# Value weights' high parts, and a third of the low parts, kept in the low 16 KB that a dead activation leaves

## The chip, the cores and the metric

The kernel runs on one core of a Trainium2 chip. The metric is the device time of one execution in microseconds (us). Three runs of the kernel before gave 1288.02, 1288.10 and 1289.45 us; their median is 1288.1 us.

## The reference

The reference is two transformer blocks over one sequence of 256 tokens, 1024 wide, in float32. The first block has sliding-window attention, a retention branch and a gated feed-forward. The second has a gated spatial unit, banded chunk attention and a PEER feed-forward: each token picks 16 of 16384 experts in each of 8 heads. Only that last part matters here. In the reference it is

```python
u = jnp.take(expert_u, eidx, axis=0)
h = jax.nn.gelu(jnp.einsum('thkd,td->thk', u, xb))
vv = jnp.take(expert_v, eidx, axis=0)
return jnp.einsum('thk,thkd->td', (g * h.astype(jnp.float32)).astype(xb.dtype), vv)
```

## The kernel before

The kernel doesn't gather experts. It computes the hidden value of every expert for every token, multiplies by a matrix that is zero where an expert was not picked, and multiplies with all of the value weights. So the PEER part is two dense layers of 128 blocks, each block with 128 experts and one 128x1024 weight tile (512 KB). The first layer (`first_layer`, L110 to L112) leaves its result in `S`, 128 blocks of 128 experts by 256 tokens. The second layer (`second_layer`, L1065) sums over the experts into four PSUM banks.

Every float32 matmul is made of three matmuls in `fp32r`. A weight is split in a high part (`whi`, made on ACT by a rounding copy, L95) and a low part (`wlo`, the rest, made on DVE, L96), an activation likewise. High by high, high by low and low by high are added up in PSUM.

In a matmul one operand is loaded into the array (the stationary one, `lhsT`, LDWEIGHTS, engine row PEld), and the other streams past it (the moving one, `rhs`). Which is which differs by stage:

- `gemm_t` (most of the program, the first PEER layer too): the weights are stationary, the activations move, 256 columns a matmul.
- `gemm_n` (some projections of both blocks): the activations are stationary, the weights move, 512 columns a matmul.
- `second_layer`: the split of `S` (tiles `keys` and `q`) is stationary, the value weights move, 512 columns a matmul. A block is 12 matmuls: for each of two token halves, `whi` by `keys`, `wlo` by `keys` and `whi` by `q`, each over two column halves. So the high part moves in 8 of them and the low part in 4.

The tiles lie along the partition, which holds 224 KB. Pools opened with the default side "right" lie at its top, the others at its bottom. As the program is built, the weights of this stage lie at the top: three buffers of `whi` from 184 KB, three of `wlo` from 196 KB, four of `raw` (the loaded weight) from 208 KB. The tiles `keys` (two) and `q` (three) lie from 178 KB. At the bottom, from 18.75 KB to 34.75 KB, lies the pool `xb`: the tiles `xbl` and `xbh`, the low and high part of the input of the first PEER layer. They are read for the last time by the last matmuls of that layer. The activations of the earlier stages (`acth`, `actl`) lie from 34.75 KB to 66.75 KB.

What sets the order: the Tile framework schedules each engine's instructions ahead of time and gives each engine a fixed list, which it works off in order. `unit` (L77) traces a weight's load, ACT copy and DVE subtraction with a raised priority, so that they are placed early, as far as a free buffer can be had for them at that place. A load is issued on SP's queue, and waits for the DVE subtraction that read the same `raw` buffer four weights before. At the seam between the layers ACT has four kinds of work in one list: weight splits (L95), the gelu of the last pair of first-layer blocks (L1003 and L1006), and the splits of `S` into `keys` (L154). PE's block j of the second layer needs `keys` and `q` of block j, and there are two `keys` buffers, so that the split of block j waits for block j-2 on PE.

Of the kernel before, what the change touches and what calls it, by code (L numbers as in the profile page):

```python
# [8 lines left out]
F32R = mybir.dt.float32r  # L9
# [34 lines left out]
class Net:  # L44
# [29 lines left out]
            self.wraw = self.pool(name + "r", raw, stack)  # L74
        self.wpools.append(self.pool(name + "p", parts, stack))

    def unit(self, src, n, pieces=1, engine=None, between=None):  # L77
        with self.tc.high_priority(offset=AHEAD):
            return self.unit_(src, n, pieces, engine, between)

    def unit_(self, src, n, pieces, engine, between):
        nc = self.nc
        self.turn += 1
        wpar = self.wpools[self.turn % len(self.wpools)]
        raw = self.wraw.tile([128, 1024], F32, name="raw")
        hi = wpar.tile([128, 1024], F32R, name="whi")
        lo = wpar.tile([128, 1024], F32R, name="wlo")
        for i in range(pieces):
            s = slice(i * n // pieces, (i + 1) * n // pieces)
            nc.sync.dma_start(out=raw[:, s], in_=src[:, s])  # L90
            if between and i:
                between(i)
        for i in range(pieces):
            s = slice(i * n // pieces, (i + 1) * n // pieces)
            self.last_copy = nc.scalar.activation(hi[:, s], raw[:, s], AF.Copy).ins  # L95
            low = (engine or nc.vector).tensor_tensor(out=lo[:, s], in0=raw[:, s], in1=hi[:, s].bitcast(F32),  # L96
                                                      op=OP.subtract)
            if engine is None:
                self.last_low = low.ins
        return hi, lo  # L100
# [616 lines left out]
    def peer(self, st, x3, h, acc):  # L717
        nc, a, tc = self.nc, self.a, self.tc
# [296 lines left out]
        def fetch(j):  # L1015

            C = gp.tile([128, 4, 128], F32, name="C", bufs=3)
            i = nc.gpsimd.dma_start(out=C, in_=cview[:, j:j + 4]).ins
            for o in put_by:
                tc.add_manual_dep(i, o.name, after, reason="all heads have been added")  # L1020
            return C

        def apply(j, C):
            with tc.issue_after(self.last_low):
                nc.vector.tensor_tensor(out=S[:, j:j + 4, TH:], in0=S[:, j:j + 4, TH:], in1=C, op=mult)
# [34 lines left out]
        def second_layer(j, tb, w, s, dhs):  # L1060
            ts = slice(tb * 128, tb * 128 + 128)
            for dh in dhs:
                for left, right, first, end in ((0, 0, j == 0, False), (0, 1, False, False), (1, 0, False, j == 127)):
                    for d in dh:
                        nc.tensor.matmul(banks[tb][d], lhsT=s[left][:, ts], rhs=w[right][:, d * 512:d * 512 + 512],  # L1065
                                         start=first, stop=end)

        held = []
        for j in range(128):
            w = self.unit(a["peer_v"][j], 1024)  # L1070
            s = [qp.tile([128, T], F32R, tag=t, name=t, bufs=n) for t, n in (("keys", 2), ("q", 3))]
            self.split(S[:, j], s[0], s[1])
            if j < 126:
                for tb in range(2):
                    second_layer(j, tb, w, s, ((0, 1),))
            else:
                held.append((j, w, s))
            if j % 4 == 0 and j < 124:
                apply(j + 4, fill.pop(0))
                if j < 116:  # L1080
                    fill.append(fetch(j + 12))
            if j == 120:
                groups.close()
                with tc.using_default_side("right"):
                    x3 = self.pool("x3", 1).tile([128, 2, D], F32, name="x3")
                nc.sync.dma_start(out=x3, in_=x3t.rearrange("b t d -> t b d"))
# [94 lines left out]
```

## Time and profile before

| | us |
|---|---|
| median of three runs | 1288.1 |
| the profiled execution | 1288.32 |
| its span | 1286.5 |
| PE busy | 1276.2 |
| DVE busy | 904.6 |
| ACT busy | 719.0 |
| the second PEER layer, first to last matmul start | 934.20 to 1282.15 |

The profile is one execution. The span is from the first to the last thing it shows; what lies outside of it is 1.8 us here. Engines are PE (matmul), PEld (loading the stationary operand), DVE, ACT, POOL and SP (which issues the loads). A timeline row has the start in us, the time it took in us, the engine, the line, the operation, and what is written and read. In brackets stands how long the engine was idle before it, and whom it waited for. PE's matmuls overlap in the rows, since each is shown until its last result is out. So the pace of PE is read from the distance of their starts, not from the time that one takes.

### The profile page before, as it was taken

Reading aid. Unit: us, or ns where it says so; the run is one execution under the profiler, and the core shown is the slowest. Engines: PE = TensorE matmul, PEld = TensorE weight load, DVE = VectorE, ACT = ScalarE, POOL = GpSimd, SP = SyncE. Lnnn points to the kernel's source line nnn. Section 1 sums busy time; section 2 is a strip of 40 time slices with the busy share of each in tenths; the row PEclk is TensorE's granted clock in tenths of the full one; section 3 lists DMA queues with packets and bytes.
Section 4 is the critical chain, followed back from the end, with each engine's and each line's share of the span. In section 5 each row is a group of like instructions: output and inputs, shape, how many; then the busy total and the mean of one; then the engine's idle time right before and its main releaser. Section 6 shows DMA issues by size and latency. Waiting matters only on the chain.

```text
span 1286.5 us, 23584 instructions
## 1 busy us (share of the span) xinstructions
PE 1276.2 (99%) x9125; PEld 1187.6 (92%) x9125; DVE 904.6 (70%) x1790; ACT 719.0 (56%) x1163; POOL 259.8 (20%) x173
## 2 busy tenths in 40 slices
PE   8999999999999999999999999999999999999998
PEld 8878999999999889999999999999988888888887
DVE  6767677766665887997995666666566666666665
ACT  5455545544454776645556666665555555555553
POOL 2000000000000000037787777770000000000000
PEclk8999999999999999999999999999999999999999
DMA  7745668966567444568777777775777777777764
GB/s 261 231 137 158 179 186 296 338 185 192 171 188 225 148 148 146 186 169 198 172 181 192 174 177 169 177 171 175 216 218 220 217 217 217 219 219 219 217 201 158
DMA packets 90928, 253.02 MB, mean 197 GB/s; under 512 B 26944, under 2 KB 28736, under 8 KB 90688
## 3 DMA queue, kind: packets, MB, share of 16 engines
q1 hardware_dynamic: 68816, 241.45, 61.0%
q0 software_dynamic: 20992, 8.46, 5.9%
q8 instruction: 71, 1.16, 0.4%
q10 hardware_dynamic: 1008, 1.61, 0.4%
q14 instruction: 41, 0.34, 0.1%
HBM read 240.93 MB, written 10.55 MB: 195 GB/s over the span
## 4 chain that ended last, share of the span: by engine, by line
PE 94%; DVE 3%; DMA 1%; issue 0%; POOL 0%; ACT 0%; SPq 0%; ACTq 0%; POOLq 0%; DVEq 0%
PE ax L1065 27%; PE mm L110 21%; PE mm L111 21%; PE mm L112 21%; DVE wlo L96 1%; PE ax L942 1%; DMA raw<-in_w_in_a_dram 1%; PE ax L888 0%; DMA xT<-in_xT_dram 0%; DVE itop L741 0%; PE ax L678 0%; PE ax L713 0%; PE ax L478 0%; PE ax L466 0%; PE ax L700 0%
## 5 line engine op out<-in xcount | busy, mean ns | idle before, releaser
L96 DVE TENSOR_TENSOR wlo<-raw,whi 128x1024 fp32r<-128x1024 f32 (+2 forms) x433 | 524.4, 1213 | 232.6 <-ACT whi L95 230.1
L95 ACT ACTIVATE whi<-raw 128x1024 fp32r<-128x1024 f32 (+3 forms) x439 | 457.6, 1045 | 306.2 <-PE mm L111 210.4
L110 PE MATMUL mm<-xbh,whi 128*128 128x256 f32 x1104 | 312.6, 283 | 0.0
L112 PE MATMUL mm<-xbh,wlo 128*128 128x256 f32 x1104 | 308.0, 279 | 1.7 <-DVE wlo L96 1.5
L111 PE MATMUL mm<-xbl,whi 128*128 128x256 f32 x1104 | 308.2, 279 | 0.0
L832 POOL DMA_INDIRECT cmat<-best,pos x128 | 232.1, 1813 | 219.1 <-DVE itop L741 155.4
L110 PE MATMUL mm<-acth,whi 128*128 128x256 f32 x848 | 240.2, 283 | 1.8 <-ACT acth L252 1.0
L111 PE MATMUL mm<-actl,whi 128*128 128x256 f32 x848 | 238.6, 281 | 0.7 <-DVE actl L253 0.6
L112 PE MATMUL mm<-acth,wlo 128*128 128x256 f32 x848 | 237.8, 280 | 0.0
L112 PEld LDWEIGHTS mm<-xbh,wlo 128*128 128x128 f32 x1104 | 207.4, 188 | 2.3 <-DVE wlo L96 2.3
L110 PEld LDWEIGHTS mm<-xbh,whi 128*128 128x128 f32 x1104 | 207.5, 188 | 0.2
L111 PEld LDWEIGHTS mm<-xbl,whi 128*128 128x128 f32 x1104 | 207.6, 188 | 0.0
L110 PEld LDWEIGHTS mm<-acth,whi 128*128 128x128 f32 x848 | 160.7, 190 | 2.9 <-ACT acth L252 1.2
L111 PEld LDWEIGHTS mm<-actl,whi 128*128 128x128 f32 x848 | 160.7, 189 | 1.6 <-DVE actl L253 1.5
L112 PEld LDWEIGHTS mm<-acth,wlo 128*128 128x128 f32 x848 | 160.8, 190 | 0.2 <-DVE wlo L96 0.2
L1065 PE MATMUL ax<-whi,keys 128*128 128x512 f32 x512 | 158.0, 389 | 0.0
L1065 PE MATMUL ax<-wlo,keys 128*128 128x512 f32 x512 | 157.9, 389 | 0.0
L1065 PE MATMUL ax<-whi,q 128*128 128x512 f32 x512 | 157.9, 389 | 0.0
L154 ACT ACTIVATE keys<-S 128x256 fp32r<-128x256 f32 x128 | 53.4, 418 | 151.4 <-PE ax L1065 151.4
L1065 PEld LDWEIGHTS ax<-wlo,keys 128*128 128x128 f32 x512 | 96.1, 188 | 20.0
L1065 PEld LDWEIGHTS ax<-whi,q 128*128 128x128 f32 x512 | 96.1, 188 | 19.9
L1065 PEld LDWEIGHTS ax<-whi,keys 128*128 128x128 f32 x512 | 96.0, 188 | 19.9
(282 smaller groups left out, 1409.1 us busy)
## 6 DMA issues: line engine op xcount, KB each, us to landing
raw<-in_peer_u_dram SPq DMA_DIRECT2D x128, 512.0 KB
raw<-in_peer_v_dram SPq DMA_DIRECT2D x128, 512.0 KB
raw<-in_w_in_b_dram SPq DMA_DIRECT2D x32, 512.0 KB
raw<-in_w_in_a_dram SPq DMA_DIRECT2D x31, 512.0 KB
raw<-in_w_gate_dram SPq DMA_DIRECT2D x22, 512.0 KB
raw<-in_w_up_dram SPq DMA_DIRECT2D x22, 512.0 KB
raw<-in_w_out_dram SPq DMA_DIRECT2D x16, 512.0 KB
cmat<-zero SPq DMA_DIRECT2D x16, 512.0 KB
```

The lines of the kernel that those rows point to most:

```text
L95: self.last_copy = nc.scalar.activation(hi[:, s], raw[:, s], AF.Copy).ins
L96: low = (engine or nc.vector).tensor_tensor(out=lo[:, s], in0=raw[:, s], in1=hi[:, s].bitcast(F32), op=OP.subtract)
L110: mm(ps, lhsT=left[0], rhs=right[0], start=first, stop=False)
L111: mm(ps, lhsT=left[0], rhs=right[1], start=False, stop=False)
L112: mm(ps, lhsT=left[1], rhs=right[0], start=False, stop=last)
L154: nc.scalar.activation(hi, src, AF.Copy)
L832: i = nc.gpsimd.indirect_dma_start(self.cmat, bass.IndirectOffsetOnAxis(ap=ps[:, hd, 1, k:k + 1], axis=0), bs[:, hd, 1, k:k + 1], None, co ...
L942: nc.tensor.matmul(C[:, t * 128:t * 128 + 128], lhsT=A[:, t], rhs=G[i][:, t], start=i == 0, stop=i == 1)
L1065: nc.tensor.matmul(banks[tb][d], lhsT=s[left][:, ts], rhs=w[right][:, d * 512:d * 512 + 512], start=first, stop=end)
```

## The change

From block 3 of the second layer on, the tiles for the weights' high part are no longer taken from the pool at the top. `xbl` and `xbh` are taken again under the name `under`, as two tiles of 2 x 1024 columns, which gives four places of 4 KB. The high part of block j goes to place j modulo 3. The low part goes to the fourth place when j is a multiple of 3, and to the three buffers of the pool otherwise.

```diff
-    def unit_(self, src, n, pieces, engine, between):
+    def unit_(self, src, n, pieces, engine, between, hi=None, lo=None):
...
-        hi = wpar.tile([128, 1024], F32R, name="whi")
-        lo = wpar.tile([128, 1024], F32R, name="wlo")
+        if hi is None:
+            hi = wpar.tile([128, 1024], F32R, name="whi")
+        if lo is None:
+            lo = wpar.tile([128, 1024], F32R, name="wlo")
...
         for j in range(128):
-            w = self.unit(a["peer_v"][j], 1024)
+            if j == 3:
+                under = [self.xbp.tile([128, 2, 1024], F32R, tag=t, name="under", bufs=1) for t in ("xbl", "xbh")]
+                under = [x[:, i] for x in under for i in range(2)]
+            place = {"hi": under[j % 3], "lo": None if j % 3 else under[3]} if j >= 3 else {}
+            w = self.unit(a["peer_v"][j], 1024, **place)
```

The order of ACT's list moves at the seam of the two layers. `whi_12041` is the high part of block 2, and `whi_12063` and `whi_12085` those of blocks 3 and 4; `gt_11985` and the row after it are the gelu of the last pair of the first layer; `keys_12046` is the split of `S` for block 2, `keys_12068` for block 3. Before:

```order
L95 ACTIVATE whi_12041<-raw_12040 128x1024
L1003 ACTIVATE gt_11985<-mm_11924 128x256
L1006 ACTIVATE S_6237<-mm_11924 128x2x128
L154 ACTIVATE keys_12046<-S_6237 128x256
L95 ACTIVATE whi_12063<-raw_12062 128x1024
L154 ACTIVATE keys_12068<-S_6237 128x256
L95 ACTIVATE whi_12085<-raw_12084 128x1024
```

With the change (its lines stand 2 lower in the file; `raw_12064`, `raw_12084` and `raw_12108` are the loaded weights of blocks 3, 4 and 5):

```order
L97 ACTIVATE whi_12041<-raw_12040 128x1024
L97 ACTIVATE under_12062<-raw_12064 128x1024
L97 ACTIVATE under_12062<-raw_12084 128x1024
L97 ACTIVATE under_12063<-raw_12108 128x1024
L1005 ACTIVATE gt_11985<-mm_11924 128x256
L1008 ACTIVATE S_6237<-mm_11924 128x2x128
L156 ACTIVATE keys_12046<-S_6237 128x256
L156 ACTIVATE keys_12068<-S_6237 128x256
```

The high parts of blocks 3, 4 and 5 have moved ahead of the gelu and of the split for block 2. Before, they stood behind it, one after each split.

On DVE, at the same seam, the rows behind the low part of block 2 (`wlo_12042`) were these before; `q_12047` is the low part of the split of `S` for block 2:

```order
L96 TENSOR_TENSOR wlo_12042<-raw_12040,whi_12041 128x1024
L1004 TENSOR_TENSOR S_6237<-S_6237,gt_11985 128x2x128
L155 TENSOR_TENSOR q_12047<-S_6237,keys_12046 128x256
L96 TENSOR_TENSOR wlo_12064<-raw_12062,whi_12063 128x1024
L155 TENSOR_TENSOR q_12069<-S_6237,keys_12068 128x256
```

and are these with the change:

```order
L98 TENSOR_TENSOR wlo_12042<-raw_12040,whi_12041 128x1024
L98 TENSOR_TENSOR under_12063<-raw_12064,under_12062 128x1024
L98 TENSOR_TENSOR wlo_12085<-raw_12084,under_12062 128x1024
L1006 TENSOR_TENSOR S_6237<-S_6237,gt_11985 128x2x128
L157 TENSOR_TENSOR q_12047<-S_6237,keys_12046 128x256
```

The low parts of blocks 3 and 4 have moved ahead of the gelu's product and of `q` for block 2. From block 7 on both engines alternate weight split and split of `S` as before. PE's list is the same matmul for matmul; only the places that they read differ.

## Rows read from the trace of the kernel before

**Rows 1.** The page: its head, the busy times and the chain that ended last.

```profile
span 1286.5 us, 23584 instructions
...
PE 1276.2 (99%) x9125; PEld 1187.6 (92%) x9125; DVE 904.6 (70%) x1790; ACT 719.0 (56%) x1163; POOL 259.8 (20%) x173
...
PE 94%; DVE 3%; DMA 1%; issue 0%; POOL 0%; ACT 0%; SPq 0%; ACTq 0%; POOLq 0%; DVEq 0%
PE ax L1065 27%; PE mm L110 21%; PE mm L111 21%; PE mm L112 21%; DVE wlo L96 1%; PE ax L942 1%; DMA raw<-in_w_in_a_dram 1%; PE ax L888 0%; DMA xT<-in_xT_dram 0%; DVE itop L741 0%; PE ax L678 0%; PE ax L713 0%; PE ax L478 0%; PE ax L466 0%; PE ax L700 0%
```

**Rows 2.** Windows of the second layer: stretch, busy us (instructions) by engine, PEclk.

```profile
940.00:1275.00 335.00, 335.00 (x1480) 277.39 (x1479) 218.64 (x277) 182.50 (x247) 14.48 (x27) 1.00 0.71 214
```

**Rows 3.** Groups by line, 940 to 1275 us: busy us, mean ns, idle before.

```profile
L1065 PE MATMUL ax<-whi,keys 128*128 128x512 f32 x494 | 152.2, 389 | 0.0
L1065 PE MATMUL ax<-wlo,keys 128*128 128x512 f32 x494 | 152.1, 389 | 0.0
...
L96 DVE TENSOR_TENSOR wlo<-raw,whi 128x1024 fp32r<-128x1024 f32 x123 | 150.7, 1226 | 79.3 <-ACT whi L95 79.3
```

**Rows 4.** Timeline of ACT in the second layer: splits of S, fourteen blocks apart.

```profile
1200.53 0.42 ACT L154 ACTIVATE keys<-S 128x256 fp32r<-128x256 f32 x1 [1.21 <-PE ax L1065]
...
1238.61 0.42 ACT L154 ACTIVATE keys<-S 128x256 fp32r<-128x256 f32 x1 [1.21 <-PE ax L1065]
```

**Rows 5.** Timeline of PE, first and last of the program's last six matmuls.

```profile
1281.02 0.39 PE L1065 MATMUL ax<-whi,keys 128*128 128x512 f32 x1
...
1282.15 0.39 PE L1065 MATMUL ax<-whi,q 128*128 128x512 f32 x1
```

**Rows 6.** Timeline of PE in gemm_n, first and last of seventeen matmuls.

```profile
99.74 0.40 PE L111 MATMUL mm<-wlo,acth 128*128 128x512 f32 x1
...
103.47 0.40 PE L112 MATMUL mm<-whi,actl 128*128 128x512 f32 x1
```

**Rows 7.** Timeline of PE in gemm_t, first and last of 33 matmuls.

```profile
147.79 0.28 PE L110 MATMUL mm<-acth,whi 128*128 128x256 f32 x1
...
151.52 0.28 PE L112 MATMUL mm<-acth,wlo 128*128 128x256 f32 x1
```

**Rows 8.** Timeline of PE, later in gemm_t, first and last of 28 matmuls.

```profile
299.80 0.28 PE L110 MATMUL mm<-acth,whi 128*128 128x256 f32 x1
...
302.98 0.28 PE L110 MATMUL mm<-acth,whi 128*128 128x256 f32 x1
```

**Rows 9.** Timeline of ACT at the seam of the two layers.

```profile
934.28 1.06 ACT L95 ACTIVATE whi<-raw 128x1024 fp32r<-128x1024 f32 x1 [1.74 <-PE mm L111]
935.25 0.36 ACT L1003 ACTIVATE gt<-mm 128x256 f32<-128x256 f32 x1
935.51 0.38 ACT L1006 ACTIVATE S<-mm 128x256 f32<-128x256 f32 x1
936.69 0.42 ACT L154 ACTIVATE keys<-S 128x256 fp32r<-128x256 f32 x1 [0.80 <-PE ax L1065]
937.14 1.06 ACT L95 ACTIVATE whi<-raw 128x1024 fp32r<-128x1024 f32 x1
939.41 0.42 ACT L154 ACTIVATE keys<-S 128x256 fp32r<-128x256 f32 x1 [1.20 <-PE ax L1065]
```

**Rows 10.** Timeline of PE at the seam: the first two matmuls of the second layer.

```profile
934.20 0.63 PE L1065 MATMUL ax<-whi,keys 128*128 128x512 f32 x2
```

**Rows 11.** Timeline of DVE at the seam: the low part of block 1.

```profile
932.58 1.23 DVE L96 TENSOR_TENSOR wlo<-raw,whi 128x1024 fp32r<-128x1024 f32 x1 [0.64 <-ACT whi L95]
```

**Rows 12.** Timeline of SP: issue of the loads of blocks 4 and 5.

```profile
931.03 0.33 SPq L90 DMA_DIRECT2D raw<-in_peer_v_dram  x1
...
933.83 0.33 SPq L90 DMA_DIRECT2D raw<-in_peer_v_dram  x1
```

**Rows 13.** The chain in order of time: loads of weights at the start (start us, us).

```profile
9.15 5.44 DMA raw<-in_w_in_a_dram
...
20.21 4.50 DMA raw<-in_w_in_a_dram
```

More of the change, by code (lines that the diff above doesn't have):

```diff
@@ L75, in weights, with unit @@
         self.wpools.append(self.pool(name + "p", parts, stack))
-    def unit(self, src, n, pieces=1, engine=None, between=None):
+    def unit(self, src, n, pieces=1, engine=None, between=None, hi=None, lo=None):
         with self.tc.high_priority(offset=AHEAD):
-            return self.unit_(src, n, pieces, engine, between)
-    def unit_(self, src, n, pieces, engine, between):
+            return self.unit_(src, n, pieces, engine, between, hi, lo)
+    def unit_(self, src, n, pieces, engine, between, hi=None, lo=None):
         nc = self.nc
```

## The prediction

> **What bounds the kernel now.** I read the page first. PE is busy for 99% of the span, and the chain that ended last is 94% PE, 27% of it in line 1065, the second PEER layer [rows 1]. So what counts is whether PE waits, and how fast it runs where it doesn't. The second layer answers the first: from 940 to 1275 us PE is busy for all of 335 us, DVE for 219 and ACT for 183, at a granted clock of 1.00, which is the 2.4 GHz level [rows 2]. No matmul of line 1065 had idle time before it [rows 3]. Giving weights more buffers can bring nothing there.
>
> The second question is the pace. In the timeline, ACT's splits of `S` come once a block, since each waits for PE. Fourteen blocks take 1238.61 - 1200.53 = 38.08 us [rows 4], 2.720 us a block, 226.7 ns for each of 12 matmuls. 512 columns at 2.4 GHz are 213.3 ns, so each matmul has a surcharge of 13.4 ns. Over 1536 matmuls that is 20.6 us, and it is all that a change of places could act on. The three kinds of matmul have the same mean of 389 ns whether the high or the low part moves [rows 3]. At the program's end, where no weight is loaded or split any more, six matmuls still start 1.13 us / 5 = 226 ns apart [rows 5]. So neighbours' traffic isn't what sets the surcharge.
>
> Other stages have other surcharges. In `gemm_n`, where the same weight buffers move 512 columns but the stationary operand lies at the bottom, sixteen steps take 3.73 us, 233.1 ns each: 19.8 ns over 213.3 [rows 6]. In `gemm_t`, where the moving operand lies at the bottom and the stationary one at the top, 32 steps of 256 columns take 3.73 us, 116.6 ns each: 9.9 over 106.7 [rows 7]. Later, with the same names, 27 steps take 3.18 us, 117.8 ns each, 11.1 over [rows 8].
>
> **The change part by part.** It adds and removes no instruction. Loads, splits and matmuls stay as many and as large; where they write and read changes, and the order on ACT and DVE at the seam.
>
> *The seam.* ACT now has the high parts of blocks 3, 4 and 5 ahead of the gelu and of the split `keys` for block 2, and it works in order. Block 2's copy starts at 934.28 as before; its wait is for PE's last use of its old buffer [rows 9]. Block 3 follows at once. The load of block 4 was issued at 931.03, that of block 5 only at 933.83, right after DVE's low part of block 1 had given its `raw` buffer back (932.58 + 1.23 = 933.81) [rows 11, 12]. A load of this size took 4.50 us on the chain at the start, and 5.44 with other loads beside it [rows 13]. So block 5's weight lands at 933.83 + 4.50 = 938.33, and ACT stands still until then. Behind it are queued the two gelu steps and `keys`. By the spacing before, copy to gelu is 0.97, gelu to its second step 0.26, that step 0.38 and `keys` 0.42 [rows 9]: `keys` is done at 938.33 + 2.03 = 940.36. PE's block 2 is due 24 matmuls after 934.20 [rows 10], at 934.20 + 24 x 0.2267 = 939.64. With a few hundredths for handing over, PE waits 0.8 us, where it waited for nothing. DVE's two low parts moved ahead are done by then: block 2's copy ends at 934.28 + 1.06 = 935.34 [rows 9], its low part 1.23 later [rows 11] at 936.57, and two more of these at 939.03, and the product after them waits for the gelu anyhow. `q` of block 2 is needed four matmuls after `keys`, 0.9 us later; I price it on DVE as `keys` on ACT, 0.42 [rows 9]. So `keys` is what ends last. Bounds: nothing, if the load takes 0.8 us less than the row; 1.7 us, with the load of 5.44. It can't be below nothing, since no work at the seam goes away. I take 0.8, by the load that ran with the fewest others beside it.
>
> SP's later loads wait for DVE's low parts as before, and those of blocks 3 and 4 come earlier now, so that no load is later. From block 7 on the lists alternate as before, with three places for the high part as before. The low part's wait for a free place changes with its places, which is worth nothing, as PE waits for neither.
>
> *The places.* From block 3 to 127, 125 blocks, 8 matmuls each move the high part: 1000. The low part lies in the fourth place in blocks 3, 6, ... 126, 42 blocks with 4 matmuls each: 168. So 1168 matmuls read the moving operand at the bottom, with the stationary one still at the top. No row shows 512 columns so. The nearest are: the same matmul at six other places, with one mean and one pace (no change, 0); `gemm_n`, the two operands at opposite ends (233.1 - 226.7 = +6.4 ns each); and `gemm_t`, the moving operand in this end but with 256 columns (9.9 - 13.4 = -3.5 ns each, if the surcharge is one per matmul). In time that is 0, 1168 x 6.4 = +7.5 us and 1168 x 3.5 = -4.1 us. I take 0: the same names have run at 116.6 and at 117.8 ns a matmul [rows 7, 8], so the surcharge moves without a change of the place, and within the second layer the six places make no difference.
>
> The Trainium skill ("TensorE: Matmul & The Clock Gate", "Back-to-back issue gap") gives an isolated warm matmul as N / 2.4 plus 2.5 ns, an estimate of 215.8 ns here; the trace's 226.7 doesn't agree, so either this data type costs more or something about the operands does. By that page all 1168 matmuls could gain 10.9 ns, 12.7 us.
>
> *Sum.* The profiled execution took 1288.32 us, 1286.5 in the span and 1.8 around it, and it lies 0.2 above the median of the runs. 1288.32 + 0.8 = 1289.1 for it, and 1288.1 + 0.8 = 1288.9 us for a median.
>
> **The rivals.** *Slower: opposite ends.* Every row where PE's two operands lie at opposite ends has a surcharge of 9.3% or more of the columns' time (19.8 of 213.3 in rows 6, 9.9 of 106.7 in rows 7), and the one stage with both at the top has 6.3%. If the ends decide, and by columns, 1168 matmuls go to 233.1 ns: +7.5 + 0.8 = +8.3, 1296.4 us. For it: `gemm_n` reads the very same weight buffers and differs in the stationary operand's place alone, and its surcharge is twice that of `gemm_t` to a tenth. Against it: rows 8 differ from rows 7 with the places' ends the same. It decides from 400 matmuls on: at 6.4 ns they make 2.6 us.
>
> *Faster: one surcharge per matmul, set by the moving operand.* Then the bottom gives `gemm_t`'s 9.9 ns: -4.1 + 0.8 = -3.3, 1284.8 us. For it: it is the lowest surcharge of these rows. Against it: `gemm_n` and the second layer move the same buffers, at 233.1 and 226.7 ns.
>
> *Much faster.* The surcharge goes altogether: 1168 x 13.4 = 15.7, less 0.8: 1273.2 us. No row shows a matmul of these types without one. The Trainium skill's figure above ("TensorE: Matmul & The Clock Gate") would lie near it.
>
> *The change does nothing to PE, and the wait isn't there either*: 1288.1, inside my case.
>
> **How the numbers follow.** The forecast has a chance of 0.37, with its own range of 1288.0 to 1290.0; opposite ends 0.34; one surcharge per matmul 0.24; much faster 0.03; 0.02 is left for what I don't see. A measurement of this kernel can tell 0.2%, 2.6 us, from no change. The forecast lies within it; opposite ends lie outside; the faster rival is just outside, at 3.3, and a part of its chance falls within. So faster 0.26, same 0.39, slower 0.35. The range from 1284.4 to 1297.6 takes in both rivals' middles and leaves out some 0.16, their far sides and the much faster case.
>
> **What would show it.** The seam: in the timeline of the changed kernel ACT stands idle before the third copy into `under`, until about 938.3, and PE has a gap of some 0.8 us before block 2, at 939.6; with no such gap that step is wrong. The places: ACT's splits of `S` 2.720 us apart in 1200 to 1240 as now. 2.76 or more speaks for the opposite ends (8 of 12 matmuls at 233.1 make 2.771), 2.70 or less for the faster rival (8 at 223.2 make 2.692), and in blocks of j divisible by 3 the step must be half as large again. Then my choice of 0 is wrong, and the time with it. Any new idle time of PE after block 6 would make the sum wrong.

## The result, and the profile after

The changed kernel takes 1296.72 us (median of 4 runs, 1296.01 to 1296.94), the one before 1288.06 us in runs beside it. The ratio is 1.0064, with a 95% interval of 1.0052 to 1.0076: 8.7 us slower. The forecast of 1288.9 us was wrong. The time lies in the range, at the number of the rival called opposite ends, 1296.4 us. The experiments show that this rival had the right rows and the wrong cause.

The page of the changed kernel (head, busy times, chain by line) answers to [rows 1]:

```profile
span 1294.2 us, 23583 instructions
...
PE 1282.5 (99%) x9125; PEld 1185.9 (92%) x9125; DVE 905.1 (70%) x1790; ACT 719.0 (56%) x1163; POOL 259.1 (20%) x173
...
PE ax L1067 27%; PE mm L112 21%; PE mm L113 21%; PE mm L114 21%; DVE wlo L98 1%; PE ax L944 1%; PE ax L890 0%; DMA raw<-in_peer_v_dram 0%; DVE itop L743 0%; DMA small<-in_small_dram 0%; ACT whi L97 0%; PE ax L680 0%; PE ax L715 0%; PE ax L480 0%; PE ax L468 0%
```

PE is busy for 6.3 us more, with as many instructions; the other engines do what they did. The window of the second layer, columns as in [rows 2]:

```profile
940.00:1275.00 335.00, 335.00 (x1446) 271.17 (x1445) 212.80 (x271) 176.67 (x239) 14.48 (x27) 1.00 0.70 212
```

Its groups by line, columns as in [rows 3]:

```profile
L1067 PE MATMUL ax<-under,keys 128*128 128x512 f32 x639 | 187.4, 395 | 0.0
L1067 PE MATMUL ax<-under,q 128*128 128x512 f32 x478 | 148.7, 392 | 0.0
...
L1067 PE MATMUL ax<-wlo,keys 128*128 128x512 f32 x322 | 101.0, 395 | 0.0
```

PE still waits for nothing and its granted clock is 1.00, but 335 us now hold 1446 of its matmuls, not 1480. So the pace fell. The timeline of PE at the first matmul of four blocks, the first of them block 96, whose number is a multiple of 3 (start, us, what):

```profile
1201.04 1.09 PE L1067 MATMUL ax<-under,keys 128*128 128x512 f32 x4
...
1203.84 0.63 PE L1067 MATMUL ax<-under,keys 128*128 128x512 f32 x2
...
1206.61 0.62 PE L1067 MATMUL ax<-under,keys 128*128 128x512 f32 x2
...
1209.39 1.09 PE L1067 MATMUL ax<-under,keys 128*128 128x512 f32 x4
```

In a block of a multiple of 3, whose 12 matmuls all move from the bottom, the step is 2.80 us, 233.3 ns a matmul. In the other two it is 2.77 and 2.78, where 8 matmuls at 233.3 and 4 at 226.7 make 2.773. That holds for the sum of a block, not matmul by matmul: in these two blocks the step after a matmul with the low part is 230.0 or 235.9 ns on average over the layer, and after one with the high part 227.6 to 235.0. ACT's splits of `S` (which answer to [rows 4]) are 38.96 us apart over 14 blocks, 2.783 us a block against 2.720:

```profile
1200.78 0.42 ACT L156 ACTIVATE keys<-S 128x256 fp32r<-128x256 f32 x1 [1.25 <-DVE wlo L98]
...
1239.74 0.42 ACT L156 ACTIVATE keys<-S 128x256 fp32r<-128x256 f32 x1 [1.25 <-DVE under L98]
```

The seam answers to [rows 9, 10, 12]. The timeline of SP, the issue of block 5's load:

```profile
933.25 0.33 SPq L92 DMA_DIRECT2D raw<-in_peer_v_dram  x1
```

Of ACT, the copy that waits for it and the split for block 2:

```profile
937.47 1.06 ACT L97 ACTIVATE under<-raw 128x1024 fp32r<-128x1024 f32 x1 [0.81 <-DMA raw<-in_peer_v_dram]
...
938.96 0.72 ACT L156 ACTIVATE keys<-S 128x256 fp32r<-128x256 f32 x2
```

Of PE, the layer's first row (0.59 us earlier than in the execution before, most of it from a stretch ahead of the layer that is looked at below, with the pad of 160 bytes), and from the last pair of block 1 on:

```profile
933.61 0.63 PE L1067 MATMUL ax<-whi,keys 128*128 128x512 f32 x2
...
938.62 0.61 PE L1067 MATMUL ax<-whi,q 128*128 128x512 f32 x2
939.43 0.73 PE L1067 MATMUL ax<-whi,keys 128*128 128x512 f32 x2 [0.19 <-ACT keys L156]
940.00 0.63 PE L1067 MATMUL ax<-wlo,keys 128*128 128x512 f32 x2
```

The next pair after 938.62 was due two steps later, at 939.07, and started at 939.43: 0.36 us late. That pair took 0.57 instead of 0.45. So the stall is real and costs 0.48 us.

The two terms account for the layer. From first to last matmul start it went from 347.95 us (934.20 to 1282.15) to 356.24 (933.61 to 1289.85), 8.29 more. 42 blocks x 0.080 + 83 x 0.053 = 7.8, and 0.48 for the seam, make 8.2.

### The profile page after: what moved, and what is told of

The parts are those of the page before. It is cut to its first block, busy times and chain, and to the rows that moved or that the text cites. A ratio compares the mean times of both kernels' runs of the same rounds, so it can differ in the third digit from the quotient of the medians.

```text
span 1294.2 us, 23583 instructions
## 1 busy us (share of the span) xinstructions
PE 1282.5 (99%) x9125; PEld 1185.9 (92%) x9125; DVE 905.1 (70%) x1790; ACT 719.0 (56%) x1163; POOL 259.1 (20%) x173
## 3 DMA queue, kind: packets, MB, share of 16 engines
q10 hardware_dynamic: 1008, 1.61, 0.3%
## 4 chain that ended last, share of the span: by engine, by line
PE 95%; DVE 4%; DMA 1%; ACT 0%; issue 0%; ACTq 0%; DVEq 0%
PE ax L1067 27%; PE mm L112 21%; PE mm L113 21%; PE mm L114 21%; DVE wlo L98 1%; PE ax L944 1%; PE ax L890 0%; DMA raw<-in_peer_v_dram 0%; DVE itop L743 0%; DMA small<-in_small_dram 0%; ACT whi L97 0%; PE ax L680 0%; PE ax L715 0%; PE ax L480 0%; PE ax L468 0%
## 5 line engine op out<-in xcount | busy, mean ns | idle before, releaser
L97 ACT ACTIVATE whi<-raw 128x1024 fp32r<-128x1024 f32 (+2 forms) x314 | 325.0, 1039 | 300.4 <-PE mm L113 210.6
L98 DVE TENSOR_TENSOR wlo<-raw,whi 128x1024 fp32r<-128x1024 f32 (+2 forms) x308 | 371.3, 1208 | 151.4 <-ACT whi L97 149.1
L1067 PE MATMUL ax<-under,keys 128*128 128x512 f32 x668 | 196.1, 394 | 0.0
L1067 PE MATMUL ax<-under,q 128*128 128x512 f32 x500 | 155.9, 392 | 0.0
L1067 PEld LDWEIGHTS ax<-under,keys 128*128 128x128 f32 x668 | 125.3, 188 | 29.0
L98 DVE TENSOR_TENSOR wlo<-raw,under 128x1024 fp32r<-128x1024 f32 x83 | 101.7, 1225 | 53.6 <-ACT under L97 53.6
L97 ACT ACTIVATE under<-raw 128x1024 fp32r<-128x1024 f32 x125 | 132.8, 1063 | 6.1 <-DMA raw<-in_peer_v_dram 0.8
L1067 PEld LDWEIGHTS ax<-under,q 128*128 128x128 f32 x500 | 93.9, 188 | 22.7
```

## The experiments

Addresses below are bytes along the partition in the built programs. What I call the distance is the address of the moving operand minus that of the stationary one, modulo 256. In the kernel before it is 0 in the second layer (weights at 188384 + multiples of 4096, `keys` and `q` at 182240 + multiples of 1024; the 512-byte halves keep it), 224 in `gemm_n` and 32 in `gemm_t` (activations at 35584). In the changed kernel `under` starts at 19200, so that its distance to `keys` is 32. I began with opposite ends (A), the moving operand's place (B), the alignment of each operand by itself (C) and a lasting state of PE (D); from the fifth run on, the distance is E.

**A bench over places.** PE alone, on twelve tiles of 16 KB, from 16.1 to 208.1 KB of the partition:

```python
for m in range(12):
    for s in range(12):
        wide(m, s, 0, 0)      # 24 matmuls of 512 columns, reg[m] moving, reg[s] stationary
```

> A bench, not the network: all weights, both blocks and the experts are left out, and PE does nothing but fp32r matmuls on tiles of ones. Twelve tiles of 16 KB (r00 to r11) fill the partition from 16.1 to 208.1 KB. Each of the 144 pairs (moving, stationary) has 24 matmuls of 512 columns in a row, then 24 of 256 columns; then r00 and r11 are paired again with the operands 0, 32 or 64 bytes off. Theory A, opposite ends: a matmul starts 226.7 ns after the last one where both tiles lie in the same half of the partition and 233.3 where they lie in different halves; the offsets change nothing. Theory C, alignment: all 144 pairs at 226.7, since all tiles have the same address modulo 64; where just one operand is 32 bytes off, 233.3. Theory D, the pace is a state of PE that lasts until it stalls: one pace from the first pair to the last.

Timeline of PE: the first row of the 512-column part, of the 256-column part, of the part with offsets, and of what follows its first nine pairs (the tiles all carry the name `r`):

```profile
20.32 5.60 PE L127 MATMUL ps<-r 128*128 128x512 f32 x24
...
803.67 3.04 PE L132 MATMUL ps<-r 128*128 128x256 f32 x24
...
1218.39 50.00 PE L127 MATMUL ps<-r 128*128 128x512 f32 x216
1268.22 99.80 PE L127 MATMUL ps<-r,r 128*128 128x512 f32 x432
```

3456 matmuls over all 144 pairs of places take 783.35 us, 226.7 ns each, and taken apart no pair differs by over 0.1 ns. So in this bench the place counts for nothing, neither the operands' ends (A) nor the moving one's place (B). With 256 columns it is 414.72 / 3456 = 120.0 ns, everywhere. In the offset part the pace changes at once, against D: the nine pairs of offsets on one tile average 49.83 / 216 = 230.7 ns. Taken apart, the three pairs with equal offsets run at 226.7; moving 64 against stationary 0 at 228.9; the other five, 0 against 64 among them, at 233.3. So 64 bytes are not the period, and alignment of each operand by itself isn't it. What counts is how the two stand to each other.

**All weights 32 bytes lower.**

```diff
+            self.pad = self.pool("pad", 1).tile([128, 8], F32, name="pad")
             self.weights("wb", self.stack, 4, 3)
```

> The kernel before with a pad of 32 bytes ahead of the pools at the top: all weights, keys and q lie 32 bytes lower, and the activations at the bottom where they were. Theory A, opposite ends: no change, 1288.1 us. Theory C, alignment modulo 64 bytes: now all operands are aligned alike, so gemm_n falls from 233.1 to 226.7 ns a matmul (some 400 matmuls, 2.5 us) and gemm_t from 116.6 or 117.8 to 113.3 (some 6500 matmuls, 3.3 to 4.4 ns each, 21 to 29 us): 1257 to 1265 us; the second PEER layer stays at 2.720 us a block.

1292.37 us, ratio 1.0035 [1.0022, 1.0047]. Both theories missed. `gemm_n`, now at a distance of 192, still took 233.3 ns. `gemm_t`, now at 64, took 117.8 nearly everywhere, and so lost the 116.7 that it had in about 4000 matmuls: 4000 x 1.1 ns = 4.4 us, near the 4.7 measured. Alignment modulo 64 fell with this.

**The stationary operand at the bottom, the moving one at the top**, from block 3 of the kernel before:

```diff
...
+                if j == 3:
+                    low = self.xbp.tile([128, 8, T], F32R, tag="xbl", name="low", bufs=1)
+                s = [low[:, j % 2], low[:, 2 + j % 3]]
```

> The kernel before, the weights of the second PEER layer left at the top, but keys and q (the stationary operand) in the dead input at the bottom from block 3 on. Theory A, opposite ends, and theory C, alignment: 12 matmuls of 233.3 ns a block, 2.800 us, 125 blocks x 0.080 = +10 us, 1298 us. Theory B, only the moving operand's place counts: 2.720 us a block as before, 1288 us.

1298.17 us, ratio 1.0083 [1.0066, 1.0100], +10.5 us. Timeline of PE, two half blocks four half blocks apart:

```profile
1199.38 1.10 PE L1065 MATMUL ax<-whi,low 128*128 128x512 f32 x4
...
1204.98 1.10 PE L1065 MATMUL ax<-whi,low 128*128 128x512 f32 x4
```

5.60 us for two blocks, 2.80 a block. The moving operand's place is the one of before, so B falls here too. Between A and a theory of distance (224 here) this run doesn't decide.

**Both at the bottom** (the high part and the split of `S`; the low part of the weights stays at the top):

```diff
...
-            place = {"hi": under[j % 3], "lo": None if j % 3 else under[3]} if j >= 3 else {}
+                under = self.xbp.tile([128, 2, 1024], F32R, tag="xbl", name="under", bufs=1)
+                low = self.xbp.tile([128, 8, T], F32R, tag="xbh", name="low", bufs=1)
+            place = {"hi": under[:, j % 2]} if j >= 3 else {}
...
+                s = [low[:, j % 2], low[:, 2 + j % 3]]
```

> The changed kernel, but the high part has two places at the bottom, the low part none, and keys and q lie at the bottom as well from block 3 on. Theories A and C: the 8 matmuls of a block with the high part have both operands at the bottom and go back to 226.7 ns, the 4 with the low part go to 233.3: 2.747 us a block, 125 x 0.027 = +3.3 us and up to 0.6 for the seam, 1291.5 to 1292 us. Theory B, only the moving operand's place counts: 8 at 233.3 and 4 at 226.7, 2.773 us a block, +6.7, 1295 us.

1292.95 us, ratio 1.0039 [1.0025, 1.0053], +5.3 us against the 1287.65 us of the kernel before beside it, in the middle between the two sums. The pieces decide. Timeline of PE in half a block, four matmuls with the high part and two with the low:

```profile
1200.77 1.07 PE L1067 MATMUL ax<-under,low 128*128 128x512 f32 x4
1201.68 0.63 PE L1067 MATMUL ax<-wlo,low 128*128 128x512 f32 x2
1202.15 1.07 PE L1067 MATMUL ax<-under,low 128*128 128x512 f32 x4
```

Four in 0.91 us are 228 ns each, where B wants 233.3; two in 0.47 are 235. Over the layer the means are 227.8 and 234.8, so each kind is some 1.3 ns slower than in an even stream. Here every half block changes the distance twice, and that seems to cost a little; in the mixed blocks of the changed kernel, which change it as often, the sum shows no such loss. Why stays open.

**The high part at the bottom, 224 bytes higher**, so that its distance is 0 as before the change (the low part stays in its pool):

```diff
...
+                under = [under[i][:, 56 + o:1080 + o] for i, o in ((0, 0), (1, 0), (1, 1024))]
+            place = {"hi": under[j % 3]} if j >= 3 else {}
```

> The changed kernel, but only the high part lies at the bottom (three places, the low part stays in its pool), and its places are 224 bytes higher, so that they have the same address as keys and q modulo 512 bytes, as the weights at the top had. Theory A, opposite ends: 8 of 12 matmuls at 233.3 ns, 2.773 us a block, +6.7 us and up to 0.6 for the seam, 1295 us. Theory E, the distance of the two operands modulo 512 bytes: 2.720 us a block as in the kernel before, and only the seam is left, up to 0.6 us: 1288.3 us.

1288.54 us against 1288.08, ratio 1.0004 [0.9994, 1.0014]. Timeline of ACT, splits of `S` fourteen blocks apart:

```profile
1201.59 0.42 ACT L156 ACTIVATE keys<-S 128x256 fp32r<-128x256 f32 x1 [1.21 <-PE ax L1067]
...
1239.67 0.42 ACT L156 ACTIVATE keys<-S 128x256 fp32r<-128x256 f32 x1 [1.21 <-PE ax L1067]
```

38.08 us, the 2.720 us a block of before, with the high part at the bottom and `keys` at the top. The change without its offset is a change that costs its seam alone, whose stall is in this trace too.

**A bench over distances**, sixteen tiles each 32 bytes further, as moving operand and in the end as stationary one, with stalls of PE put in between:

```python
for f in (narrow, wide):          # 256 columns in gemm_t's order; 512 in the second layer's
    for n in (64, 200, 333, 512):
        stall(n)                  # PE waits for a memset of n columns
        for o in off:             # off000 .. off480
            f(o)
    for n in (100, 300):
        for o in off:
            stall(n)
            f(o)
    ...
```

> A bench, not the network: PE alone, on tiles of ones, all weights left out. The tiles off000 to off480 lie 0, 32, ... 480 bytes (modulo 512) from h0 and l0. In the first part (256 columns) they move and h0 and l0 are stationary, in the order of gemm_t; in the second (512 columns) they move in the order of the second layer; each part goes through the 16 offsets six times, with a stall of PE ahead of each round or of each offset; at the end off000 to off480 are stationary and h0 moves. Theory E, the distance modulo 512 bytes sets the pace: with 512 columns 226.7 ns at 0, 228.9 at 64, and 233.3 at 32, 224 and 288, whatever came before; with 256 columns 120.0 at 0, and at 288 (as in gemm_t) 116.7 or 117.8. If the 256-column pace depends on how PE came into the stretch, the rounds at the same offset differ. Theory A, opposite ends: all 16 offsets alike.

In the rounds with 512 columns the sixteen distances give each pace twice, 0 and 256 alike, 32 and 288, and so on, so the period is 256 bytes. 0 gives 226.7, and nothing else does; 64 gives 228.8, or 233.3 after some stalls. At the end, where these tiles are stationary and the moving one stays, the tiles 192 and 448 bytes up, whose distance is 64, give 228.8 again, and a tile 64 bytes up 233.4: it is the difference of the two addresses that counts, with its sign. With 256 columns the pace depends also on how PE came in. At 192 two values hold, each to the end of its stretch. Timeline of PE at a distance of 192, fifteen groups of three matmuls in a round without stalls, then five such groups after a stall:

```profile
144.34 0.28 PE L129 MATMUL ps<-off,l 128*128 128x256 f32 x1
...
149.64 0.28 PE L129 MATMUL ps<-off,l 128*128 128x256 f32 x1
```

```profile
425.71 0.39 PE L129 MATMUL ps<-off,h 128*128 128x256 f32 x2
...
427.41 0.39 PE L129 MATMUL ps<-off,h 128*128 128x256 f32 x2
```

5.30 us / 45 = 117.8 ns and 1.70 / 15 = 113.3. At 32, `gemm_t`'s distance, it is 116.7 or 117.8 in the same way: those are [rows 7] and [rows 8].

**keys and q 32 bytes lower, all at the top**, in the kernel before:

```diff
+            self.pad = self.pool("pad", 1).tile([128, 8], F32, name="pad")
             qp = self.pool("query", 1)
```

> The kernel before with a pad of 32 bytes behind the weights at the top: keys and q stay at the top, but 32 bytes lower against the weights; the weights and the activations lie where they were. Theory A, opposite ends: no change, 1288 us. Theory E, the distance modulo 256 bytes: it is 32 in the second layer, so all 1536 matmuls take 233.3 ns, 2.800 us a block, 128 x 0.080 = +10.2 us, 1298 us; gemm_t and gemm_n as before.

1297.87 us, ratio 1.0077 [1.0061, 1.0094], +9.9 us. Timeline of ACT, splits of `S` fourteen blocks apart:

```profile
1200.48 0.42 ACT L154 ACTIVATE keys<-S 128x256 fp32r<-128x256 f32 x1 [1.27 <-DVE wlo L96]
...
1239.68 0.42 ACT L154 ACTIVATE keys<-S 128x256 fp32r<-128x256 f32 x1 [1.27 <-DVE wlo L96]
```

39.20 / 14 = 2.800 us. All at one end, and the slow pace: with the aligned high part above this is the pair that separates place and distance.

**All weights 160 and 224 bytes lower**, the diff of 32 bytes with another length:

> The kernel before with a pad of 160 bytes ahead of the pools at the top, nothing else. keys and q move with the weights, so the second layer stays at 2.720 us a block. In gemm_t the distance (moving minus stationary, modulo 256 bytes) goes from 32 to 192, in gemm_n from 224 to 64. Theory E by the bench of offsets: at 192, 256 columns take 113.3 ns where PE came in from a stall and 117.7 where it came from another offset. Before, about 4000 of the 6528 matmuls take 116.7 and 2500 take 117.8. If all go to 113.3: 4000 x 3.3 + 2500 x 4.4 = 24 us less, and gemm_n 384 x 4.5 ns = 1.7 less: 1262 us. If the slower pace of that offset holds throughout: +4 - 1.7, 1290 us. Theory A, opposite ends: no change, 1288 us.

> The same with a pad of 224 bytes: the distance is 0 in all three stages. Theory E by the bench: gemm_t at 120.0 ns, 4000 x 3.3 + 2500 x 2.2 = 19 us more; gemm_n at 226.7, 384 x 6.6 = 2.5 us less; second layer 2.720 us a block as before: 1304.5 us. Theory C, alignment modulo 64 bytes alone: gemm_t at 113.3 and 1264 us. Theory A, opposite ends: no change, 1288 us.

160 bytes: 1270.10 us, ratio 0.9884 [0.9841, 0.9926], 17.6 us faster than the kernel before. But its four runs took 1269.33, 1269.57, 1270.63 and 1280.01 us, and the time is their median. 224 bytes: 1302.70 us, ratio 1.0118 [1.0101, 1.0135]. Timeline of PE in the stretch of [rows 8], first and last of 28 matmuls, with 160 bytes, then with 224:

```profile
299.82 0.28 PE L112 MATMUL mm<-acth,wlo 128*128 128x256 f32 x1
...
302.88 0.28 PE L112 MATMUL mm<-acth,wlo 128*128 128x256 f32 x1
```

```profile
299.81 0.28 PE L112 MATMUL mm<-acth,wlo 128*128 128x256 f32 x1
...
303.05 0.28 PE L112 MATMUL mm<-acth,wlo 128*128 128x256 f32 x1
```

3.06 / 27 = 113.3 ns and 3.24 / 27 = 120.0, where [rows 8] have 117.8. With 224 bytes nearly all of `gemm_t` runs so. With 160 it holds for most; some 1200 to 1400 matmuls, most of them in stretches between 43 and 694 us, keep to the other value of that distance, 117.8. At 4.4 ns each that is 5 to 6 of the 8 us by which the time misses the sum of 1262. One of those stretches:

```profile
669.73 0.28 PE L111 MATMUL mm<-xbl,whi 128*128 128x256 f32 x1
...
672.90 0.28 PE L111 MATMUL mm<-xbl,whi 128*128 128x256 f32 x1
```

3.17 / 27 = 117.4 in these rounded rows, and 117.8 over the 430 steps of the whole stretch. This version beats both kernels.

Which pace a stretch gets is not settled by the addresses and the order of the matmuls. Up to block 3 of the second layer the kernel before and the changed one have the same matmuls at the same addresses. Timeline of PE in one stretch of both, 28 matmuls each, at the distance of 32; the kernel before, then the changed one:

```profile
669.64 0.28 PE L111 MATMUL mm<-xbl,whi 128*128 128x256 f32 x1
...
672.82 0.28 PE L111 MATMUL mm<-xbl,whi 128*128 128x256 f32 x1
```

```profile
669.60 0.28 PE L113 MATMUL mm<-xbl,whi 128*128 128x256 f32 x1
...
672.75 0.28 PE L113 MATMUL mm<-xbl,whi 128*128 128x256 f32 x1
```

3.18 / 27 = 117.8 ns and 3.15 / 27 = 116.7. The stretch goes on for 430 matmuls so, which is 0.5 of the 0.59 us by which the changed kernel came earlier to its second layer. The run of 1280.01 us with the pad may be of this kind: by an estimate from the two paces at 192, some 2300 more matmuls at 117.8 ns would take its 10 us. No trace of that run was kept, so this isn't shown.

**A bench over types.**

```python
for still, off in (half, full):          # float16, fp32r; tiles a to i, 0 to 256 bytes
    for cols in (512, 256):
        for x in off:
            run(still, x, cols)          # 48 matmuls
```

> A bench, not the network: PE alone, on tiles of ones, all weights left out. 48 matmuls for each of nine distances of the moving from the stationary operand, 0, 32, ... 256 bytes (tiles a to i), first in float16 (half), then in fp32r (full), each with 512 and then with 256 columns. Theory E1, the distance counts for every type of two or four bytes: float16 has several paces too. Theory E2, it is a matter of fp32r: float16 keeps one pace at all nine distances, about 2.4 ns over the columns' time as the network's float16 matmuls have it (215.7 ns for 512 columns, 109.1 for 256), and fp32r repeats the bench of offsets (226.7 ns at 0 and 256, 228.9 at 64, 233.3 to 234.6 elsewhere).

Timeline of PE: float16 (first two of nine), then fp32r with 512 columns, with the first row of the part behind:

```profile
19.18 10.52 PE L125 MATMUL ps<-halfa,half 128*128 128x512 f16 x48
29.54 10.52 PE L125 MATMUL ps<-halfb,half 128*128 128x512 f16 x48
39.90 10.52 PE L125 MATMUL ps<-halfc,half 128*128 128x512 f16 x48
...
159.50 11.15 PE L125 MATMUL ps<-fulla,full 128*128 128x512 f32 x48
170.49 11.37 PE L125 MATMUL ps<-fullb,full 128*128 128x512 f32 x48
181.69 11.16 PE L125 MATMUL ps<-fullc,full 128*128 128x512 f32 x48
192.69 11.37 PE L125 MATMUL ps<-fulld,full 128*128 128x512 f32 x48
203.90 11.36 PE L125 MATMUL ps<-fulle,full 128*128 128x512 f32 x48
215.10 11.40 PE L125 MATMUL ps<-fullf,full 128*128 128x512 f32 x48
226.34 11.35 PE L125 MATMUL ps<-fullg,full 128*128 128x512 f32 x48
237.53 11.35 PE L125 MATMUL ps<-fullh,full 128*128 128x512 f32 x48
248.72 11.05 PE L125 MATMUL ps<-fulli,full 128*128 128x512 f32 x48
259.61 5.92 PE L125 MATMUL ps<-fulla,full 128*128 128x256 f32 x48
```

Start to start, divided by 48: float16 takes 10.36 us a tile, 215.8 ns, at every distance. fp32r takes 229.0 (0 bytes, with the change of type in it; 226.7 once under way), then 233.3, 229.2, 233.5, 233.3, 234.2, 233.1, 233.1 and, at 256 bytes, 226.9. So the distance counts for fp32r and not for float16.

## Why the prediction failed in its likeliest case

*What bounds the kernel* was right: PE has no idle time in the layer, so its pace is the one thing that the change could touch, and every microsecond but the seam's came from there.

*The places, "I take 0".* This step failed: the term was put at 0 and measured +7.8 us. Its argument was that the same matmul runs at one pace at six places. But those six places are 4096 bytes apart, and so have one distance to `keys` and `q`, 0. The sample held constant the very thing that the change altered. The second half of the argument, that [rows 7] and [rows 8] differ with the places' ends the same, was true and spoke against ends alone; at a distance of 32 both values occur. The measured value is just beyond the other end of the bound (6.4 ns each, +7.5): 6.7 ns on average for each of the 1168 matmuls.

*Opposite ends.* The number was right (2.771 us a block and +7.5, measured 2.77 to 2.78 and 7.8), and its row was the right one: in `gemm_n` the weight buffers are the same and the stationary operand's address differs. That it lies at the other end is beside the point; that it lies 224 bytes off modulo 256 is the point. That the number held was luck: the changed kernel's distance is 32, not 224, and these two have the same pace, 233.3, while 64 would have given 228.9. The sign that the prediction set for this rival, 2.76 or more and half as much again in blocks of a multiple of 3, came true too, and could not tell the ends from the addresses. Three runs can: at 144 pairs of places there is one pace; 32 bytes at one end are worth 10 us; and at opposite ends with a distance of 0 the pace is the one of before, 2.720 us a block.

*One surcharge per matmul* and *much faster* fell with the bench: 10 ns belong to 256 columns at a distance of 32, and no even stream of fp32r matmuls of 512 columns ran faster than 226.7. The figure of the Trainium skill ("TensorE: Matmul & The Clock Gate", "Back-to-back issue gap"), N / 2.4 plus 2.5 ns for an isolated warm matmul, is met by the float16 rows above, 215.8 ns, and by none of fp32r.

*The seam* was right in kind and 0.3 us too large. The load took 937.47 - 933.25 = 4.22 us, not 4.50, and from the copy to the split for block 2 it was 1.49 us, where the spacing before gave 1.61. Even so the forecast's sum would have been right to 0.4 us at a distance of 0: that version took 1288.54.

What the runs leave open is why the distance counts, and what makes PE come into a stretch of 256 columns at one or the other pace of its distance; the stalls of the bench show that the entry matters, not how.

## What to carry to other kernels

Where fp32r matmuls fill the time, look at the addresses of the two operands modulo 256 bytes, not at where they lie: in these runs 0 was best for 512 columns, and 192 for 256 columns, where PE came into the stretch at the faster of its two paces. A pad of a few words ahead of a pool sets the distance; it does not set which of two paces a stretch gets, so take several runs. A pace that is the same in many rows proves nothing about what those rows have in common. So before a tile is moved to free room, compare the new address with the old one in its low bits.

## What the runs showed of the hardware that I had not expected

- The pace of an fp32r matmul depends on moving minus stationary address modulo 256 bytes: with 512 columns 226.7 ns at 0, 228.9 (or 233.3) at 64 and 232.4 to 234.6 elsewhere; with 256 columns 120.0 at 0 and at 96, the slowest there, and down to 113.3 at 64 and 192.
- Nothing of this shows in float16 (215.8 and 109.2 ns at nine distances), and at a distance of 0 nothing depends on the place along the partition (226.7 ns at 144 pairs of places).
- With 256 columns one distance can have two paces (116.7 and 117.8 at 32; 113.3 and 117.8 at 64 and 192), which last as long as the stream does, over 1400 matmuls in the kernel before. The same stretch of the program had one of the two in the kernel before and the other in the changed kernel.
- A pad of 160 bytes, which takes no instruction, makes this kernel 1.2% faster (interval 0.7% to 1.6%; three of its four runs 1.3 to 1.4%, one 0.6%).
